# Experts' weights in 256 x 1024 tiles, split whole, with products and evictions over two PSUM banks

## Chip, cores and metric

One core of a Trainium2 chip runs one program of two transformer blocks. The metric is the device time of one execution in microseconds; less is better. Three runs of the kernel before are shown, and one execution was profiled.

## What is computed

512 tokens of width 1024, float32, go through two blocks. The first has a recurrence, an attention and a layer of 32 experts; each token goes to its four best ones. Of an expert, the part that matters here is this:

```python
def expert_block(args):
    tok, gate, e = args
    xb = xt[tok]
    hid = xb @ w1[e] + b1[e]
    glu = jnp.minimum(hid[:, :D_FF_EXPERT], SWIGLU_LIMIT)
    lin = jnp.clip(hid[:, D_FF_EXPERT:], -SWIGLU_LIMIT, SWIGLU_LIMIT)
    act = glu * jax.nn.sigmoid(SWIGLU_ALPHA * glu) * (lin + 1.0)
    return (act @ w2[e] + b2[e]) * gate[:, None]
```

`w1[e]` is 1024 x 2048: its first 1024 columns give the gated half, the others the linear half. `w2[e]` is 1024 x 1024. Results go back to their tokens, summed. The second block is a convolution, a sparse attention and a feed-forward layer; the change leaves its code alone.

## The kernel before, in words

**Precision.** A float32 product is made of three: weights and activations are split in a high part in a shorter format and a low part, the rest, and `mm3` (L99) multiplies high by high, high by low and low by high. For weights, `split` (L104, L105) is a cast on ACT into `wh` and a subtraction on DVE, or on POOL where it is told so, into `wl`.

**Experts' stage** (`phase_b`, L991). The 12 MiB of an expert come in 12 chunks of 1 MiB: eight of `w1` and four of `w2`. A chunk is 512 rows by 512 columns, held as a raw tile `wraw` of 128 partitions by 4 k by 512. `weights` (L953) lists all 384 chunks in the order of their products: an expert's first layer, then the second layer of the expert before. In the first layer it takes gated and linear columns in turn: 512 gated columns (two chunks), 512 linear ones, then the other 512 of each.

For chunk n the loop at the end of `phase_b` splits chunk n + 3 (`ahead`), issues the load of the chunk that takes its raw tile (8 of them), makes the twelve products of chunk n, and then runs the steps that were put behind n with `after`. PE, ACT, DVE and SP keep the order in which the program is written here. `wsplit` (L112) cuts a chunk in `self.parts` = PB = 2 pieces of 128 x 1024, and there are `nhl` = 8 half tiles `wh` and `wl` each. A chunk's twelve products go to one PSUM bank: `hid` has four banks, `y` two, `tr` two.

**Steps of an expert** (`plan`, L1077; b is its first chunk, y0 the first of its second layer). The gather of the next expert's rows (`xg`) goes out behind b, and eight transposes (`turn`) stand behind b+6 and their two parts `xt` (high on ACT, low on DVE) behind b+8 as two pieces of 128 x 384. `swiglu` stands behind b+4 and b+8: for 512 columns a clip of the gated part, its activation on ACT, a clip of the linear part and their product, all 96 x 512. The result `ln` is turned in two groups of four transposes behind b+11 and b+13, with parts `at` behind b+12 and b+14. `finish` (behind y0+4) weighs the result into `ys` in two pieces, and POOL scatters the rows into `acc`. Experts 30 and 31 have steps of their own (`L30`, `LS`).

**Before the stage** `phase_r` (L736) multiplies by `w_out`, normalises (`rst`, `rsy`, `h2r`), and routes the tokens with many small DVE operations (`oh`, `pos`, `rowi`). In the same time the first three chunks of experts' weights are cast on ACT and subtracted on POOL, so that they are ready when the stage begins.

**Block 2**, which the prediction uses for comparison, makes its products with the same `mm3`: those named `mm` and `mu` in runs of 24 into one bank, and those named `ro` (`rows_out`, L1694) token tile by token tile, two k and so six products into a tile's bank, then six into the next one's.

## Time and profile before

| | |
|---|---|
| runs of the kernel before | 2618.61, 2621.24 and 2624.76 us, median 2621.24 |
| span of the profiled execution | 2621.5 us; the profile gives no other time for it |
| PE busy | 2522.1 us, 96% |
| DVE busy | 1853.1 us, 71% |
| ACT busy | 1385.9 us, 53% |
| mean granted clock of PE | 0.965 |
| bytes of weights of the experts | 384 loads of 1024 KB |

The span reaches from the first instruction to the last of one execution. It is 0.3 us above the median of the runs, so terms that are worked out on it can be set against the median directly. Busy is time in which an engine runs an instruction other than one that moves registers, signals or starts transfers.

### The profile page before, as it was taken

The numbers are of one execution on the slowest core, as the hardware profiler recorded it, in microseconds if no ns is written. First come the engines' busy times: TensorE is split into PE (matmuls) and PEld (weight loads), VectorE is DVE, ScalarE is ACT, GpSimd is POOL, SyncE is SP. The second block draws the span as 40 slices with busy tenths as digits, with TensorE's granted clock in tenths as the row PEclk, the third lists the DMA queues.
The fourth block names the chain that finished last, engine by engine and source line by source line (L and its number), as shares of the span: only waits on it lengthen the run. The fifth ranks groups of instructions, "written<-read, shape, count | busy, mean of one in ns | idle before, by whom it ended". The sixth has DMA issues, their size and how long they took to land. (4 is left out here: it accounts for less than half of the span.)

```text
span 2621.5 us, 33210 instructions
## 1 busy us (share of the span) xinstructions
PE 2522.1 (96%) x12362; PEld 1774.2 (68%) x12362; DVE 1853.1 (71%) x2631; ACT 1385.9 (53%) x1952; POOL 336.2 (13%) x316
## 2 busy tenths in 40 slices
PE   6999998879999999999999999997999999899999
PEld 2567765656666666666666666666777678688887
DVE  3346556679999999999999999996666643555522
ACT  2333455347777777677767776764445532322221
POOL 2000222214211111111121111121100000000000
PEclk7899899889999999999999999998999999899999
DMA  8473000669999999999999999984421132333332
GB/s 275 122 223 79 17 1 0 235 235 326 345 369 349 356 348 355 351 353 355 350 354 351 354 351 355 348 268 109 105 57 49 33 89 73 105 97 97 93 95 70
DMA packets 371566, 556.75 MB, mean 212 GB/s; under 512 B 13138, under 2 KB 153501, under 8 KB 371401
## 3 DMA queue, kind: packets, MB, share of 16 engines
q1 hardware_dynamic: 359808, 518.81, 58.1%
q0 software_dynamic: 11120, 34.68, 6.2%
q8 instruction: 98, 1.61, 0.3%
q10 hardware_dynamic: 473, 1.11, 0.1%
q14 instruction: 67, 0.55, 0.1%
HBM read 534.06 MB, written 20.48 MB: 212 GB/s over the span
## 5 line engine op out<-in xcount | busy, mean ns | idle before, releaser
L105 DVE TENSOR_TENSOR wl<-wraw,wh 128x1024 fp32r<-128x1024 f32 (+2 forms) x974 | 1093.5, 1159 | 297.9 <-ACT wh L104 278.7
L104 ACT CAST wh<-wraw 128x1024 fp32r<-128x1024 f32 (+1 forms) x980 | 950.7, 997 | 637.4 <-PE mm L96 232.8
L96 PE MATMUL hid<-wh,xt 128*96 128x512 f32 x2048 | 676.5, 398 | 0.0
L96 PEld LDWEIGHTS hid<-wh,xt 128*96 128x96 f32 x2048 | 331.0, 162 | 151.7 <-issue 9.9
L96 PE MATMUL hid<-wl,xt 128*96 128x512 f32 x1024 | 404.6, 395 | 0.0
L96 PE MATMUL y<-wh,at 128*96 128x512 f32 x960 | 314.7, 398 | 0.0
L96 PE MATMUL mm<-hH,wh 128*128 128x512 f32 x624 | 255.0, 409 | 6.9 <-ACT wh L104 3.5
L96 PE MATMUL mm<-hL,wh 128*128 128x512 f32 x624 | 252.5, 405 | 0.0
L96 PE MATMUL mm<-hH,wl 128*128 128x512 f32 x624 | 251.0, 402 | 0.0
L1209 POOL DMA_INDIRECT acc<-ys,tli x30 | 154.3, 5145 | 517.7 <-DVE ys L1118 499.0
L96 PEld LDWEIGHTS y<-wh,at 128*96 128x96 f32 x960 | 154.9, 161 | 78.1 <-issue 14.4
L96 PEld LDWEIGHTS hid<-wl,xt 128*96 128x96 f32 x1024 | 165.6, 162 | 59.5
L96 PE MATMUL y<-wl,at 128*96 128x512 f32 x480 | 189.1, 394 | 0.0
L96 PEld LDWEIGHTS mm<-hH,wh 128*128 128x128 f32 x624 | 119.1, 191 | 43.4 <-issue 5.7
L96 PEld LDWEIGHTS mm<-hH,wl 128*128 128x128 f32 x624 | 119.0, 191 | 30.3 <-issue 2.6
L96 PEld LDWEIGHTS mm<-hL,wh 128*128 128x128 f32 x624 | 119.1, 191 | 29.2 <-issue 3.0
L74 ACT ACTIVATE gl<-gl 96x512 f32<-96x512 f32 x64 | 40.5, 632 | 131.3 <-DVE gl L1057 131.3
L96 PEld LDWEIGHTS y<-wl,at 128*96 128x96 f32 x480 | 77.5, 161 | 29.0
L1036 POOL DMA_INDIRECT xg<-h2d,tli x32 | 30.8, 963 | 432.4 <-PE tr L1044 427.3
L96 PE MATMUL mu<-hL,wh 128*128 128x512 f32 x176 | 70.2, 399 | 0.0
L96 PE MATMUL mu<-hH,wh 128*128 128x512 f32 x176 | 69.3, 394 | 0.0
L96 PE MATMUL mu<-hH,wl 128*128 128x512 f32 x176 | 69.0, 392 | 0.0
(554 smaller groups left out, 3384.9 us busy)
## 6 DMA issues: line engine op xcount, KB each, us to landing
wraw<-in_exp_w_dram SPq DMA_DIRECT2D x384, 1024.0 KB
wraw<-in_w_in_dram SPq DMA_DIRECT2D x62, 512.0 KB
wraw<-in_ada_w_dram SPq DMA_DIRECT2D x48, 512.0 KB
wraw<-in_w_ffn_in_dram SPq DMA_DIRECT2D x44, 512.0 KB
wraw<-in_w_ffn_out_dram SPq DMA_DIRECT2D x22, 512.0 KB
wraw<-in_w_out_dram SPq DMA_DIRECT2D x4, 1024.0 KB
wraw<-in_w_o_dram SPq DMA_DIRECT2D x8, 512.0 KB
acc<-zf SPq DMA_DIRECT2D x1, 2432.0 KB
```

The costliest lines, as they stand in the source:

```text
L74: ins = self.nc.scalar.activation(out, in_, func, **kw)
L96: self.nc.tensor.matmul(out, l, r, start=start, stop=stop, skip_group_check=True)
L104: self.nc.scalar.copy(h, src)
L105: (eng or self.nc.vector).tensor_sub(l, src, h.bitcast(F32))
L1036: self.gathered = nc.gpsimd.indirect_dma_start(out=xg, out_offset=None, in_=self.h2d, in_offset=bass.IndirectOffsetOnAxis(ap=self.tli[:, e ...
L1209: self.nc.gpsimd.indirect_dma_start(out=self.acc, out_offset=bass.IndirectOffsetOnAxis(ap=idx, axis=0), in_=ys, in_offset=None, compute_op ...
```

## The change

Loads: experts 0 to 29 (`OLD` = 30) take chunks of 256 rows by 1024 columns, a raw tile of 128 x 2 x 1024. First come the four chunks of the gated half, then the four of the linear half, then the four of the second layer of the expert before. Experts 30 and 31 keep the old form and order of chunks.

Splits: PB is 1, so a chunk is split whole, 128 x 2048 at a time, into four tiles of twice the size; `ahead` stays 3. This also holds for the first three chunks on POOL, for `w_out` in `phase_r`, and for experts 30 and 31.

Products: for each of two k, three products into one bank and three into the other, in PSUM tiles of two banks (pool `psp`: one `tr`, two `hid`, one `y`).

Evictions: one operation over both banks. The clip and activation of the gated half stand behind b+4, the linear half's clip and the product behind b+8, both 96 x 1024. `ln` is turned whole behind b+11, and its parts, 128 x 768, stand behind b+12. `xt`'s parts are 128 x 768 too, and `ys` is 96 x 1024 in one. Biases are split in three pieces instead of five (`BS`), and the rows of the gate go to one pair. The old pool `psb` is opened after the loop. The diff, without the lines that are only comments:

```diff
 GO = 0
+OLD = 30
...
-PB = 2
+PB = 1
...
-MB = dict(xg=1,xt=1,at=1,gl=2,ln=2,ys=1,raw=7,hl=4)
+MB = dict(xg=1,xt=1,at=1,gl=1,ln=1,ys=1)
...
-BS = [0,2,4,6,8,10]
+BS = [0,1,3,10]
...
-        L1 = lambda e: [(e, 1, hb, m, kh) for hb in range(2) for m in range(2) for kh in range(2)]
-        L2 = lambda e: [(e, 2, kh, cb, 0) for kh in range(2) for cb in range(2)]
+        L1 = lambda e: [(e, 1, i) for i in range(8)]
+        L2 = lambda e: [(e, 2, i) for i in range(4)]
         seq = self.seq = []
         for e in range(NE):
             seq += L1(e) + (L2(e - 1) if e else [])
...
     def load(self, n):
         if n < len(self.seq):
-            e, layer, u, v, kh = self.seq[n]
-            if layer == 1:
-                src = self.a["exp_w1"][0][e, 512 * kh:512 * kh + 512, 512 * u + D * v:512 * u + D * v + 512]
+            e, layer, i = self.seq[n]
+            w = self.a["exp_w1" if layer == 1 else "exp_w2"][0][e]
+            if e < OLD:
+                v, kq = divmod(i, 4)
+                src, shape = w[256 * kq:256 * kq + 256, D * v:D * v + D], [128, 2, D]
             else:
-                src = self.a["exp_w2"][0][e, 512 * u:512 * u + 512, 512 * v:512 * v + 512]
+                hb, m, kh = (i // 4, i // 2 % 2, i % 2) if layer == 1 else (i % 2, 0, i // 2)
+                c0 = 512 * hb + D * m
+                src, shape = w[512 * kh:512 * kh + 512, c0:c0 + 512], [128, 4, 512]
             two = n % RAW >= self.nraw
-            w = self.raw[n] = (self.wp2 if two else self.wp).tile([128, 4, 512], F32, name="wraw", tag="wraw",
+            w = self.raw[n] = (self.wp2 if two else self.wp).tile(shape, F32, name="wraw", tag="wraw",
                                                                   bufs=RAW - self.nraw if two else self.nraw)
             self.nc.sync.dma_start(w, src.rearrange("(k p) c -> p k c", p=128))
...
-        psum = self.pool(PS, "psb", space=PSUM)
-        P = lambda tag, bufs: psum.tile([128, 512], F32, name=tag, tag=tag, bufs=bufs)
-        T_ = lambda tag, n=512: bp.tile([C, n], F32, name=tag, tag=tag, bufs=MB[tag])
+        PP = ExitStack()
+        pairs = self.pool(PP, "psp", space=PSUM)
+        P2 = lambda tag: pairs.tile([128, 2, 512], F32, name=tag, tag=tag, bufs=2 if tag == "hid" else 1)
+        T_ = lambda tag: bp.tile([C, D], F32, name=tag, tag=tag, bufs=MB[tag])
...
-        def turn(src, b, c0):
-            p = P("tr", 2)
-            for k in range(4):
-                nc.tensor.transpose(p[:, k * C:(k + 1) * C], src[:, c0 + k * 128:c0 + (k + 1) * 128], self.ident[:C, :C])
-            return p[:, 0:4 * C].rearrange("p (k c) -> p k c", c=C), slice(4 * b, 4 * b + 4)
-        def parts(t, dst, scale=1.0):
-            pv, ks = t
-            self.act(dst[0][:, ks, :], pv, AF.Copy, scale=scale)
-            nc.vector.scalar_tensor_tensor(dst[1][:, ks, :], pv, scale, dst[0][:, ks, :].bitcast(F32), op0=OP.mult, op1=OP.subtract)
+        def turn(src, p, b0, nb):
+            for k in range(4 * b0, 4 * (b0 + nb)):
+                nc.tensor.transpose(p[:, k // 4, k % 4 * C:(k % 4 + 1) * C], src[:, k * 128:(k + 1) * 128], self.ident[:C, :C])
+            return p
+        def parts(p, dst, b0, nb, scale=1.0):
+            pv = p[:, b0:b0 + nb, 0:4 * C]
+            h, l = (t[:, 4 * b0:4 * (b0 + nb), :].rearrange("p (b k) c -> p b (k c)", b=nb) for t in dst)
+            self.act(h, pv, AF.Copy, scale=scale)
+            nc.vector.scalar_tensor_tensor(l, pv, scale, h.bitcast(F32), op0=OP.mult, op1=OP.subtract)
...
+        def glu(gl, pg):
+            nc.vector.tensor_scalar(gl, flat(pg), 7.0, None, op0=OP.min)
             self.act(gl, gl, AF.Silu, scale=1.702)
-            ln = T_("ln")
-            nc.vector.tensor_scalar(ln, pl[:C], 7.0, -7.0, op0=OP.min, op1=OP.max)
+        def lin(ln, pl, gl):
+            nc.vector.tensor_scalar(ln, flat(pl), 7.0, -7.0, op0=OP.min, op1=OP.max)
             self.last = nc.vector.scalar_tensor_tensor(ln, ln, 1.0, gl, op0=OP.add, op1=OP.mult)
-            return ln
+        def swiglu(e, u):
+            if not u:
+                X["gl"], X["ln"] = T_("gl"), T_("ln")
+            cs, p = slice(512 * u, 512 * u + 512), X["hid", e, u]
+            glu(X["gl"][:, cs], p[:, 0])
+            lin(X["ln"][:, cs], p[:, 1], X["gl"][:, cs])
...
-            b, y0 = at_[(e, 1, 0, 0, 0)], at_[(e, 2, 0, 0, 0)]
+            b, y0 = at_[(e, 1, 0)], at_[(e, 2, 0)]
             if e + 1 < NE:
                 after(b, keep(("xg", e + 1), lambda: gather(e + 1)))
                 n = b + XN if e == NE - 2 else b + 6
+                after(n, keep(("tx", e + 1), lambda: turn(X["xg", e + 1], P2("tr"), 0, 2)))
+                after(n + 1 if e == NE - 2 else max(min(at_[e + 1, 1, 0], b + 12) - ahead - 1, b + 7),
+                      lambda: (X.__setitem__(("xt", e + 1), pair("at" if e == NE - 2 else "xt")),
+                               parts(X["tx", e + 1], X["xt", e + 1], 0, 2)))
+            if e < OLD:
+                after(b + 4, lambda: (X.__setitem__("gl", T_("gl")), glu(X["gl"], X["hid", e, 0])))
+                after(b + 8, lambda: (X.__setitem__("ln", T_("ln")), lin(X["ln"], X["hid", e, 1], X["gl"])))
+                after(b + 11, keep("t", lambda: turn(X["ln"], P2("tr"), 0, 2)))
+                after(b + 12, lambda: (X.__setitem__(("at", e), pair("at")), parts(X["t"], X["at", e], 0, 2, 1 / 1.702)))
+            else:
+                steps = LS if e == NE - 1 else L30
+                after(b + 4, lambda: swiglu(e, 0))
+                after(b + steps[0], lambda: swiglu(e, 1))
                 for q in range(2):
-                    after(n, keep(("tx", e + 1, q), lambda q=q: turn(X["xg", e + 1], q, 512 * q)))
-                after(n + 1 if e == NE - 2 else max(min(at_[e + 1, 1, 0, 0, 0], b + 12) - ahead - 1, b + 7),
-                      lambda: (X.__setitem__(("xt", e + 1), pair("at" if e == NE - 2 else "xt")),
-                               [parts(X["tx", e + 1, q], X["xt", e + 1]) for q in range(2)]))
-            steps = LS if e == NE - 1 else L30 if e == NE - 2 else (8, 11, 12, 13, 14)
-            after(b + 4, keep(("ln", 0), lambda: swiglu(*X["hid", e, 0])))
-            after(b + steps[0], keep(("ln", 1), lambda: swiglu(*X["hid", e, 1])))
-            for q in range(2):
-                after(b + steps[1 + 2 * q], keep(("t", q), lambda q=q: turn(X["ln", q], q, 0)))
-                after(b + steps[2 + 2 * q], lambda q=q: (q or X.__setitem__(("at", e), pair("xt" if e >= NE - 2 else "at")),
-                                                         parts(X["t", q], X["at", e], 1 / 1.702)))
+                    after(b + steps[1 + 2 * q], keep("t", lambda q=q: turn(X["ln"], X["t"] if q else P2("tr"), q, 1)))
+                    after(b + steps[2 + 2 * q], lambda q=q: (q or X.__setitem__(("at", e), pair("xt")),
+                                                             parts(X["t"], X["at", e], q, 1, 1 / 1.702)))
...
-            ys = T_("xg" if e == NE - 2 else "ys", D)
-            for cb in range(2):
-                weigh(ys[:, 512 * cb:512 * cb + 512], e, cb)
+            ys = T_("xg" if e == NE - 2 else "ys")
+            weigh(ys, e, flat(X["y", e]))
...
-            e, layer, u, v, kh = seq[n]
+            e, layer, i = seq[n]
             if layer == 1:
-                if u == 0 and v == 0 and kh == 0:
+                if i == 0:
                     plan(e)
-                if v == 0 and kh == 0:
-                    X["hid", e, u] = [P("hid", 4), P("hid", 4)]
-                p, xt, bias = X["hid", e, u][v], X["xt", e], b1s[:, D * v + 512 * u:D * v + 512 * u + 512]
+                if i % 4 == 0:
+                    X["hid", e, i // 4] = P2("hid")
+                p, xt, b0 = X["hid", e, i // 4], X["xt", e], b1s
             else:
-                if u == 0 and v == 0:
-                    X["y", e] = [P("hid", 4) if e >= NE - YH else P("y", 2) for _ in range(2)]
-                p, xt, kh, bias = X["y", e][v], X["at", e], u, b2s[:, 512 * v:512 * v + 512]
+                if i == 0:
+                    X["y", e] = P2("hid" if e >= NE - YH else "y")
+                p, xt, b0 = X["y", e], X["at", e], b2s
             w = hl.pop(n)
-            for k in range(4):
-                kk = 4 * kh + k
-                self.mm3(p[:C], (xt[0][:, kk, :], xt[1][:, kk, :]), w[k], kk == 0, False)
-            if kh:
-                mm(p[:C], e2[:, e:e + 1].to_broadcast([64, C]), bias, False, True)
+            if e < OLD:
+                v, kq = divmod(i, 4)
+                todo_ = [(2 * kq + k, j, [t[:, 512 * j:512 * j + 512] for t in w[k]], D * v + 512 * j)
+                         for k in range(2) for j in range(2)]
+            else:
+                u, j, kh = (i // 4, i // 2 % 2, i % 2) if layer == 1 else (0, i % 2, i // 2)
+                todo_ = [(4 * kh + k, j, w[k], 512 * u + D * j if layer == 1 else 512 * j) for k in range(4)]
+            for kk, j, wk, c0 in todo_:
+                self.mm3(p[:C, j], (xt[0][:, kk, :], xt[1][:, kk, :]), wk, kk == 0, False)
+                if kk == KD - 1:
+                    mm(p[:C, j], e2[:, e:e + 1].to_broadcast([e2.shape[0], C]), b0[:, c0:c0 + 512], False, True)
```

Three places where instructions move.

POOL, where the first three chunks are split (`wl<-wraw,wh`; behind them the transfer of the normalised rows to `h2d` and the first gather `xg`). Before:

```order
L105 TENSOR_TENSOR wl<-wraw,wh 128x1024 x6
L882 DMA h2d<-h2r 128x1024 x2
L1036 DMA xg<-h2d,tli 96x1024
L1106 CAST tlc<-tli 96x1
L1036 DMA xg<-h2d,tli 96x1024 x3
```

Now:

```order
L106 TENSOR_TENSOR wl<-wraw,wh 128x2048 x3
L883 DMA h2d<-h2r 128x1024 x2
L1043 DMA xg<-h2d,tli 96x1024
L1126 CAST tlc<-tli 96x1
L1043 DMA xg<-h2d,tli 96x1024 x3
```

Six subtractions of 128 x 1024 have become three of 128 x 2048; what stands behind them is the same.

ACT in `phase_r`, second half of the routing (`h2r` sums of squares, `rsy` the root, `gt` the gates, `wh` the cast of the third chunk). Before:

```order
L888 COPY h2T<-tr 128x512
L74 ACTIVATE h2r,ss_4170<-x 128x512
L104 CAST wh<-wraw 128x1024
L74 ACTIVATE rsy<-rsv 128x1
L74 ACTIVATE rsy<-rsy 128x1
L104 CAST wh<-wraw 128x1024
L888 COPY h2T<-tr 128x512 x2
L74 ACTIVATE h2r,ss_4294<-x 128x512
```

Now:

```order
L889 COPY h2T<-tr 128x512
L75 ACTIVATE h2r,ss_4154<-x 128x512
L75 ACTIVATE rsy<-rsv 128x1
L75 ACTIVATE rsy<-rsy 128x1
L105 CAST wh<-wraw 128x2048
L889 COPY h2T<-tr 128x512 x2
L75 ACTIVATE h2r,ss_4270<-x 128x512
```

Half of the third chunk's cast stood ahead of the two `rsy`; now the whole cast stands behind them.

DVE, one expert in the middle of the stage (`ys` the weighing, `at` and `xt` the low parts, `gl` and `ln` the clips and the product). Before:

```order
L1118 SCALAR_TENSOR_TENSOR ys<-y,tlg,g2b 96x512 x2
L1050 SCALAR_TENSOR_TENSOR at_9326<-tr,at_9325 128x384
L105 TENSOR_TENSOR wl<-wraw,wh 128x1024 x4
L1050 SCALAR_TENSOR_TENSOR at_9326<-tr,at_9325 128x384
L105 TENSOR_TENSOR wl<-wraw,wh 128x1024 x4
L1057 TENSOR_SCALAR gl<-hid 96x512
L1060 TENSOR_SCALAR ln<-hid 96x512
L1061 SCALAR_TENSOR_TENSOR ln<-ln,gl 96x512
L105 TENSOR_TENSOR wl<-wraw,wh 128x1024 x8
L1050 SCALAR_TENSOR_TENSOR xt_9539<-tr,xt_9538 128x384 x2
L1057 TENSOR_SCALAR gl<-hid 96x512
L1060 TENSOR_SCALAR ln<-hid 96x512
```

Now:

```order
L1139 SCALAR_TENSOR_TENSOR ys<-y,tlg,g2b 96x1024
L1057 SCALAR_TENSOR_TENSOR at_10439<-tr,at_10438 128x768
L106 TENSOR_TENSOR wl<-wraw,wh 128x2048 x4
L1065 TENSOR_SCALAR gl<-hid 96x1024
L106 TENSOR_TENSOR wl<-wraw,wh 128x2048 x4
L1057 SCALAR_TENSOR_TENSOR xt_10607<-tr,xt_10606 128x768
L1069 TENSOR_SCALAR ln<-hid 96x1024
L1070 SCALAR_TENSOR_TENSOR ln<-ln,gl 96x1024
L106 TENSOR_TENSOR wl<-wraw,wh 128x2048 x4
```

A piece is twice as long and there are half as many; the clip of the gated half stands alone, four chunks ahead of the linear half's clip and the product, and the turned `at` comes in one piece behind `ys`.

## Rows read from the trace of the kernel before

**Rows 1.** The page, its head and the first row of its part 1: busy us and share.

```profile
span 2621.5 us, 33210 instructions
...
PE 2522.1 (96%) x12362; PEld 1774.2 (68%) x12362; DVE 1853.1 (71%) x2631; ACT 1385.9 (53%) x1952; POOL 336.2 (13%) x316
```

**Rows 2.** Table by windows, core 0: window, its us, busy us of each engine, clock, DMA.

```profile
700.00:800.00 100.00, 100.00 (x442) 65.69 (x440) 93.60 (x97) 71.28 (x80) 20.45 (x5) 1.00 1.05 367
```

**Rows 3.** List of waits, 700 to 1700 us: us in total, times, longest us.

```profile
ACT wh L104 <- PE hid L96: 140.3, 290, 1.0
ACT gl L74 <- DVE gl L1057: 102.4, 52, 2.1
```

**Rows 4.** Timeline of PE, two experts' turns: start us, us, operation.

```profile
1027.65 0.82 PE L1044 MATMUL tr<-ident,xg 96*128 96x96 f32 x8
1028.26 0.45 PE L96 MATMUL hid<-wh,xt 128*96 128x512 f32 x1
...
1065.71 0.82 PE L1044 MATMUL tr<-ident,xg 96*128 96x96 f32 x8
```

**Rows 5.** The chain that ended last, block 2: start us, us, what.

```profile
2273.10 5.60 PE mm L96 x24
...
2497.10 119.73 PE ro L96 x528
```

**Rows 6.** Groups by line and form, 700 to 1700 us: busy us, mean ns of one.

```profile
L105 DVE TENSOR_TENSOR wl<-wraw,wh 128x1024 fp32r<-128x1024 f32 x634 | 745.2, 1221 | 70.8 <-ACT wh L104 66.1
L104 ACT CAST wh<-wraw 128x1024 fp32r<-128x1024 f32 x633 | 643.0, 1048 | 187.6 <-PE hid L96 140.3 <-ACT wh L104 36.1 <-PE y L96 9.7
...
L1061 DVE SCALAR_TENSOR_TENSOR ln<-ln,gl 96x512 f32<-96x512 f32 x52 | 35.8, 688 | 5.4
...
L74 ACT ACTIVATE gl<-gl 96x512 f32<-96x512 f32 x52 | 32.9, 632 | 102.4 <-DVE gl L1057 102.4
...
L1050 DVE SCALAR_TENSOR_TENSOR at<-tr,at 128x384 fp32r<-128x384 f32 x54 | 29.3, 543 | 0.0
...
L74 ACT ACTIVATE at<-tr 128x384 fp32r<-128x384 f32 x54 | 26.0, 482 | 0.0
```

**Rows 7.** Timeline of POOL, 511 to 536 us.

```profile
512.48 10.29 POOL L105 TENSOR_TENSOR wl<-wraw,wh 128x1024 fp32r<-128x1024 f32 x4 [1.83 <-ACT wh L104]
527.73 4.82 POOL L105 TENSOR_TENSOR wl<-wraw,wh 128x1024 fp32r<-128x1024 f32 x2 [4.95 <-ACT wh L104]
```

**Rows 8.** Timeline of DVE, 511 to 537 us.

```profile
520.56 2.23 DVE L847 TENSOR_TENSOR pos<-tf,pos 128x4 f32<-128x4 f32 x1
...
527.48 0.16 DVE L847 TENSOR_TENSOR pos<-tf,pos 128x4 f32<-128x4 f32 x1
...
528.03 2.22 DVE L260 TENSOR_TENSOR rst<-rsy 128x1 f32<-128x1 f32 x1
530.28 2.29 DVE L261 TENSOR_TENSOR rst<-rst,rsv 128x1 f32<-128x1 f32 x1
...
534.31 1.23 DVE L881 TENSOR_TENSOR h2r<-h2r,s 128x1024 f32<-128x1024 f32 x1
```

**Rows 9.** Timeline of ACT, 511 to 537 us.

```profile
511.35 1.05 ACT L104 CAST wh<-wraw 128x1024 fp32r<-128x1024 f32 x1 [1.08 <-PE o L96]
```

**Rows 10.** Timeline of PE, the first products of the stage.

```profile
558.21 0.74 PE L96 MATMUL hid<-wh,xt 128*96 128x512 f32 x1
558.75 0.63 PE L96 MATMUL hid<-wl,xt 128*96 128x512 f32 x1
559.17 1.05 PE L96 MATMUL hid<-wh,xt 128*96 128x512 f32 x2
```

**Rows 11.** Timeline of PE, expert 2's turn.

```profile
609.47 0.55 PE L1044 MATMUL tr<-ident,xg 96*128 96x96 f32 x4 [1.17 <-DVE at L1050]
```

**Rows 12.** Timeline of all engines, end of the stage.

```profile
1769.93 0.55 DVE L1050 SCALAR_TENSOR_TENSOR xt<-tr,xt 128x384 fp32r<-128x384 f32 x1
...
1771.69 0.62 PE L96 MATMUL hid<-wh,xt 128*96 128x512 f32 x2
```

More of the change, by code (lines that the diff above doesn't have):

```diff
@@ L1005, in phase_b @@
         bp = self.pool(ES, "moe", side="right")
[L1006 to L1008 removed]
+        PP = ExitStack()
+        pairs = self.pool(PP, "psp", space=PSUM)
+        P2 = lambda tag: pairs.tile([128, 2, 512], F32, name=tag, tag=tag, bufs=2 if tag == "hid" else 1)
+        T_ = lambda tag: bp.tile([C, D], F32, name=tag, tag=tag, bufs=MB[tag])
         braw = {}
         def bias_load():
[L1013 to L1015 removed]
+            for n, (src, c0, tag) in enumerate((("exp_b1", 0, "gl"), ("exp_b1", D, "ln"), ("exp_b2", 0, "ys"))):
+                t = T_(tag)
                 for h in range(2):
[L1017 to L1018 removed]
+                    nc.sync.dma_start(t[32 * h:32 * h + 32], a[src][0, :, c0:c0 + D])
+                braw[n] = t, (b1s if n < 2 else b2s)[:, c0:c0 + D]
         def bias_split(n):
@@ L1025, in gate_rows @@
         def gate_rows():
+            p = P2("tr")
             for j in range(2):
-                p = P("tr", 2)
-                mm(p, self.ones[32 * j + 64:32 * j + 65, :], self.mod[2][32 * j + 64:32 * j + 65, :])
-                nc.scalar.copy(g2[:, 512 * j:512 * j + 512], p[:C])
+                mm(p[:, j], self.ones[32 * j + 64:32 * j + 65, :], self.mod[2][32 * j + 64:32 * j + 65, :])
+            nc.scalar.copy(g2, p[:C].rearrange("p j c -> p (j c)"))
         self.table("silu_and_others")
@@ L1102, in onehot @@
         def onehot():
-            io, t = T_("gl"), bp.tile([C, 1], F32, name="tlc")
+            io, t = T_("gl")[:, 0:T], bp.tile([C, 1], F32, name="tlc")
             nc.gpsimd.iota(io, pattern=[[1, T]], base=0, channel_multiplier=0, allow_small_or_imprecise_dtypes=True)
@@ L1112, in last @@
                 X["ys"] = self.wp.tile([C, 4, 512], F32R, name="ysp", tag="wraw", bufs=self.nraw)
-            ys = T_("ln")
-            weigh(ys, NE - 1, cb)
-            self.split(X["ys"][:, cb], X["ys"][:, 2 + cb], ys)
-        def weigh(ys, e, cb):
-            nc.vector.scalar_tensor_tensor(ys, X["y", e][cb][:C], self.tlg[:, e:e + 1], g2[:, 512 * cb:512 * cb + 512],
-                                           op0=OP.mult, op1=OP.mult)
+                X["yr"] = T_("ln")
+            cs = slice(512 * cb, 512 * cb + 512)
@@ L1121, in finish, with weigh @@
+            weigh(X["yr"][:, cs], NE - 1, X["y", NE - 1][:C, cb], cs)
+            self.split(X["ys"][:, cb], X["ys"][:, 2 + cb], X["yr"][:, cs])
+        def weigh(ys, e, p, cs=slice(0, D)):
+            nc.vector.scalar_tensor_tensor(ys, p, self.tlg[:, e:e + 1], g2[:, cs], op0=OP.mult, op1=OP.mult)
         def finish(e):
-            ys = T_("xg" if e == NE - 2 else "ys", D)
-            for cb in range(2):
-                weigh(ys[:, 512 * cb:512 * cb + 512], e, cb)
+            ys = T_("xg" if e == NE - 2 else "ys")
+            weigh(ys, e, flat(X["y", e]))
@@ L1150, in phase_b @@
             bias_load()
-            for n in range(5):
+            for n in range(3):
                 after(BS[n], lambda n=n: bias_split(n))
-            after(BS[5], gate_rows)
+            after(BS[3], gate_rows)
             X["xg", 0], X["xt", 0] = gather(0), pair("xt")
@@ L1156, in phase_b @@
                 split(n, nc.gpsimd)
-            for q in range(2):
-                parts(turn(X["xg", 0], q, 512 * q), X["xt", 0])
+            parts(turn(X["xg", 0], P2("tr"), 0, 2), X["xt", 0], 0, 2)
             for n in range(len(seq)):
@@ L1174, in phase_b @@
         ES.close()
+        PP.close()
+        psum = self.pool(PS, "psb", space=PSUM)
+        P = lambda tag, bufs: psum.tile([128, 512], F32, name=tag, tag=tag, bufs=bufs)
         self.overflow(P)
```

12 lines of the change are left out of this document (2 added, 10 removed).

## The prediction

> **What bounds the kernel now.** I read the page first: PE is busy for 2522.1 of 2621.5 us, 96%; no other engine comes near [rows 1]. A share over the whole program says nothing of one stage, so the next view is the table by windows. The change lives in the experts' stage, which runs from about 558 to 1780 us, and there a window of 100 us has 100.00 us of PE at a granted clock of 1.00 (the 2.4 GHz level), with DVE at 94 and the DMA engines at 1.03 of their time [rows 2]. Three resources look full. The list of waits tells which of them is waited for. Between 700 and 1700 us it has no wait of PE for data and no wait for a transfer. ACT waits 290 times for PE to give back a split tile [rows 3]: the engines that prepare weights run ahead until the tiles are full, and then wait for PE. A full DMA share is a queue that is always fed, not a bound. So this stage costs what PE's instructions cost, and the questions are whether PE's list gets shorter, whether a product gets quicker or slower, and whether DVE or ACT, now with other piece sizes, ever comes late.
>
> PE's list of one expert is 144 products, six bias products and sixteen transposes. The transposes of two neighbouring experts start at 1027.65 and 1065.71 us, so an expert lasts 38.06 us and a chunk of twelve products 3.17 us on average [rows 4].
>
> **The change, part by part. Products over two banks.** Number and size of PE's instructions stay; what is new is that the bank changes after every three products instead of after twelve (or more). The rows that are nearest are in the chain of block 2: 528 products of `ro` in 119.73 us are 226.8 ns each, and in that loop the bank changes after every six; 24 products of `mm`, which stay much longer in one, are 5.60 us, 233 ns each [rows 5]. The engine pays nothing visible for a change of bank; I take 0. The ends: if all of the 6.5 ns between the two were due to banks, and the same fell to each of the 4320 products of experts 0 to 29, it would be -28 us; 5 ns lost at each of 1440 changes would be +7. That the two loops differ in much else (weights' width, other engines' load) is why neither end is my value.
>
> **Transposes in eights, biases one product earlier.** The same instructions stand grouped otherwise; the work of PE is equal, 0, between -0.3 and +0.3 us an expert by the 0.61 us from the eight transposes' start to the next product's [rows 4], which would be 9 us either way over 30 experts. I keep 0, since eight in one place already cost as much as two groups of four.
>
> **Splits in whole tiles.** DVE's time for one piece: 512 elements cost 688 ns and 1024 cost 1221 [rows 6], that is 1.04 ns an element, so 2048 are 1221 + 1024 x 1.04 = 2.29 us (ends: 2.24, and 2.44, twice a half). ACT: 632 ns for 512 and 1048 for 1024 give 0.81 ns an element, 1.88 us for 2048 (at most 2.10). The evictions over two banks are 96x1024: 688 + 533 = 1.22 us for each of the two clips, the product with the gate and `ys`; the turned parts, 128x768, 543 + 400 = 0.94 us on DVE and 0.80 on ACT. DVE per expert: 12 x 2.29 + 4 x 1.22 + 2 x 0.94 = 34.2 us of 38.06. DVE stays below PE, and its 94% falls to 90.
>
> What matters more is when a piece is ready. There are four whole tiles, as much memory as eight halves, so the cast for the chunk three ahead begins when PE leaves a tile, 3 x 3.17 = 9.5 us before that chunk's products. With nothing in the way the low part is ready after 1.88 + 2.29 = 4.2 us: 5.3 us to spare. Two places of an expert are tighter. After b+4, ACT's order puts the activation of the gated half behind DVE's clip, and the clip stands behind a whole subtraction: cast to 1.9, subtraction to 4.2, clip to 5.4, activation (about 1.05) to 6.4, next cast to 8.3, its subtraction to 10.6, needed at 12.7: 2.1 us to spare. After b+8, DVE does the turned `xt`, the clip and the product with the gate (0.94 + 1.22 + 1.22) between two subtractions: ready at 9.9, needed at 12.7, 2.8 to spare. Nothing reaches PE, so this term is 0; what covers it is those 2 us. The 102.4 us that ACT now waits for DVE's `gl` [rows 3] grow per wait and halve in number. Of the larger loads nothing is waited for today, and the bytes are the same.
>
> **The start.** Before the stage the first three chunks are cut with POOL doing the subtraction, beside DVE's routing work. The rows show a collision: POOL is at it for 10.29 and 4.82 us [rows 7], and inside these stretches DVE's operations with two inputs in SBUF stretch: `pos`, 0.16 us at 527.48, took 2.23 at 520.56, and two `rst` took 2.22 and 2.29 [rows 8], each about one POOL piece. With whole pieces POOL's are 4.8 us. The Trainium skill's page "SBUF — State Buffer" (section "SBUF: two separate sides") says that such a DVE operation and a GpSimd one that reads SBUF take a port pair as an exclusive lock for the whole instruction; the rows above agree with it, and by it a whole piece holds DVE off for up to twice as long at once, while sharing by bandwidth would leave this term near 0.
>
> First stretch: the first cast now needs a whole tile and starts about 1.4 us later than 511.35 [rows 9], ends 0.8 us later still, and POOL's two pieces end about 2.2 us after the old 522.77; DVE leaves the stretch that much later. Second stretch: ACT's order now has both `rsy` activations ahead of the whole cast, where one half stood before them. So the two `rst`, which lose 2.22 + 2.29 - 2 x 0.16 = 4.2 us today, run ahead of POOL. But POOL then starts about when `h2r` times `s` (1.23 us, at 534.31) is due, and may hold it for its 4.8 us. Held: +2.2 + 0.4 = +2.6; not held: +2.2 - 4.2 = -2.0. The two come within 0.1 us of a tie, and I think held is somewhat likelier, since POOL gets in between two DVE operations in the rows too (POOL's second piece starts between the two `rst`). I take +2.0, ends -2.0 and +2.6.
>
> **The first products** (558.21) come behind one ACT part of 0.80 us over all eight transposes instead of one of 0.48 over four: +0.5 us (0.3 to 1.1) [rows 10]. **A stall that goes:** at 609.47 PE waited for a `tr` bank [rows 11], where expert 2's transposes needed one that the turned `ln` still held. The turn is now whole after b+11, and its bank is read before the gather's turn is due: -1.4 us with the transposes' own slip. Late next would be the splits, and they have their 2 us. **The tail:** with experts 30 and 31 whole splits stand ahead of the small steps; the last low part was there at 1770.48 and products that use it begin some 1.4 us later [rows 12]; a half more ahead of it costs 0 to 1.5, I take +0.8.
>
> **Sum:** 0 + 0 + 0 + 2.0 + 0.5 - 1.4 + 0.8 = +1.9 us. The profiled execution spans 2621.5 us, 0.3 above the median of 2621.24, so the forecast is **2623 us**; the term is under 0.1% of the time. A measurement of this kernel can tell about 0.2%, 5.2 us, from no change.
>
> **Rivals.**
> - *Late splits (slower).* One mechanism: the chain clip, activation, cast, subtraction after b+4, which has 2.1 us to spare. For it: DVE would have two idle stretches less to catch up in, and the activation waits behind a piece of twice the length. Against it: waits of ACT for PE show that today's reserve is not used up. It decides once the chain takes 2.1 us more than worked out, for instance with pieces at 2.44 and 2.10 us (2 x 0.15 + 2 x 0.22 = 0.7 us) and 1.4 us of semaphores. Each 0.1 us beyond that costs 30 x 0.1 = 3 us; a lateness of 0.2 to 1 us gives 2629 to 2653. Chance 0.17.
> - *Quicker products (faster).* If the change of bank is what makes `ro` 226.8 ns, products fall from 233 towards that: -28 us, 2595; a third of it 2613. Against it: two loops are compared that differ in more. Chance 0.08.
> - *The start falls well (faster).* Not held, and first products on time: -2.0 + 0.3 - 1.4 + 0 = -3.1, 2618; it is inside the 0.2%. Part of the forecast's chance, 0.17 of it.
> - *The clock falls.* At the first products the clock was low: they start 0.54 and 0.42 us apart, against 0.23 later [rows 10]. If changing banks broke PE's run so that ten products of each expert went at that pace, 30 x 10 x 0.2 = 60 us, 2683. The windows say 1.00 throughout, and `ro` changes banks at full pace. Chance 0.03. The Trainium skill's page "TensorE: Matmul & The Clock Gate" (section "A second HAM failure mode: psum-queue depth-cycling") describes a kernel whose clock swung because PE idled a little between groups of products as it went round the banks; no run here shows that.
> - *It does nothing:* all terms 0, 2621.5; not to be told apart from the forecast, and counted with it.
>
> **How the numbers follow.** The forecast with its near cases (nothing, a start that falls well) has 0.69, late splits 0.17, quicker products 0.08, the clock 0.03, and bank changes that cost 5 ns each (+7 us) 0.03. Of the 0.69, 0.05 is for small gains that sum to over 5.2 us and 0.02 for small losses that do; of the late splits 0.03 is for a lateness so small that it lands inside. Faster: 0.08 + 0.05 = 0.13. Slower: 0.17 - 0.03 + 0.03 + 0.03 + 0.02 = 0.22. The same: 0.65. The range of 8 in 10 takes the forecast's ends (the start's -2.0 to +2.6, the tail, the first products: 2617 to 2626) and reaches to a third of the product gain below and to a lateness of about 0.4 us an expert above: 2613 to 2635.
>
> **What would show it.** Right: windows of 100 us between 700 and 1700 still with 100.00 of PE and transposes 38.0 us apart; `wl` 128x2048 near 2.29 us, `wh` near 1.88; no `tr` wait near 608; POOL's three pieces near 4.8 us with DVE operations of up to 4.8 us beside them; the first product within 3 us of 558.7. Wrong: PE waiting for `wl` or `wh` in the list of waits (late splits), an expert of 37.3 us or less (quicker products), or a granted clock below 1.00 after 600 us.

## The result, and the profile after

The changed kernel takes 2643.11 us (median of 4 runs, 2640.06 to 2646.94) against 2623.0 us before on the same chip (4 runs, 2618.61 to 2628.09): a ratio of 1.0079, 95% interval 1.0058 to 1.0100. It is slower by 15 to 26 us. The prediction was 2623, 2613 to 2635, "the same" at 0.65; it is wrong.

The page after, its head and the first row of part 1, against [rows 1]; then the table by windows, one row of the steady stage, against [rows 2]; then groups by line and form between 700 and 1700 us, against [rows 6]:

```profile
span 2638.1 us, 31763 instructions
...
PE 2526.6 (96%) x12362; PEld 1775.1 (67%) x12362; DVE 1795.2 (68%) x2061; ACT 1325.8 (50%) x1469; POOL 264.4 (10%) x313
```

```profile
700.00:800.00 100.00, 100.00 (x436) 65.48 (x435) 90.21 (x50) 64.95 (x39) 14.51 (x5) 1.00 1.00 369
```

```profile
L106 DVE TENSOR_TENSOR wl<-wraw,wh 128x2048 fp32r<-128x2048 f32 x316 | 712.3, 2286 | 122.0 <-ACT wh L105 120.3
L105 ACT CAST wh<-wraw 128x2048 fp32r<-128x2048 f32 x316 | 598.0, 1908 | 250.8 <-PE hid L97 118.2 <-PE y L97 103.6 <-issue 29.0
...
L75 ACT ACTIVATE gl<-gl 96x1024 f32<-96x1024 f32 x26 | 27.6, 1061 | 90.7 <-DVE gl L1065 90.7
```

The steady stage is as forecast: PE 100.00 of 100 us at a granted clock of 1.00, a whole subtraction 2286 ns (2.29 was worked out), a cast 1908 ns (1.88), an activation over two banks 1061, and DVE busy for 90 us of the window instead of 94. Yet the span is 16.6 us longer than the 2621.5 of before. So the loss is not in the steady part, and the next step is to cut the stage in pieces at marks that both programs have: the first of the eight transposes of an expert's gathered rows, and the first product behind the stage (`ysp`). PE's timeline before:

```profile
580.64 0.83 PE L1044 MATMUL tr<-ident,xg 96*128 96x96 f32 x8
...
607.80 0.49 PE L1044 MATMUL tr<-ident,xg 96*128 96x96 f32 x4
...
647.20 0.82 PE L1044 MATMUL tr<-ident,xg 96*128 96x96 f32 x8
...
1673.98 0.82 PE L1044 MATMUL tr<-ident,xg 96*128 96x96 f32 x8
...
1731.09 0.82 PE L1044 MATMUL tr<-ident,xg 96*128 96x96 f32 x8
...
1780.97 2.27 PE L96 MATMUL hid<-ysp,one 96*128 96x512 f32 x8 [2.39 <-issue]
```

and after:

```profile
583.66 0.82 PE L1050 MATMUL tr<-ident,xg 96*128 96x96 f32 x8
...
615.02 0.83 PE L1050 MATMUL tr<-ident,xg 96*128 96x96 f32 x8
...
653.12 0.82 PE L1050 MATMUL tr<-ident,xg 96*128 96x96 f32 x8
...
1681.78 0.82 PE L1050 MATMUL tr<-ident,xg 96*128 96x96 f32 x8
...
1745.96 0.82 PE L1050 MATMUL tr<-ident,xg 96*128 96x96 f32 x8
...
1798.07 2.12 PE L97 MATMUL hid<-ysp,one 96*128 96x512 f32 x8 [2.31 <-POOL cz L1518]
```

(At 607.80 only the first four of expert 2's transposes stand together, before the stall of [rows 11].) The differences of these starts, and three ways ahead of them, read from the same timelines:

| way | before | after | change |
|---|---|---|---|
| `w_out`'s first product (473.37; 474.66) to the last `tl` (550.41; 551.90) | 77.04 | 77.24 | +0.20 |
| last `tl` to the first turn (556.73; 558.88) | 6.32 | 6.98 | +0.66 |
| first turn to the first product (558.21; 561.32) | 1.48 | 2.44 | +0.96 |
| expert 1's turn to expert 2's | 27.16 | 31.36 | +4.20 |
| expert 2's to expert 3's | 39.40 | 38.10 | -1.30 |
| expert 3's to expert 30's, 27 experts | 1026.78 | 1028.66 | +1.88 |
| expert 30's to expert 31's | 57.11 | 64.18 | +7.07 |
| expert 31's to the first product behind the stage | 49.88 | 52.11 | +2.23 |

With -0.1 from the first product to expert 1's turn and -0.5 behind the stage these are +15.3 us; the other 1.3 us of the 16.6 fall ahead of `w_out`, in code that is the same. Two ways hold most of it.

**Expert 1.** PE's timeline after, around its first products:

```profile
588.52 0.47 PE L97 MATMUL hid<-wh,xt 128*96 128x512 f32 x1 [0.27 <-ACT xt L75]
588.83 0.40 PE L97 MATMUL hid<-wl,xt 128*96 128x512 f32 x1
591.37 0.71 PE L97 MATMUL hid<-wh,xt 128*96 128x512 f32 x2 [2.15 <-DVE xt L1057]
...
592.15 1.04 PE L97 MATMUL hid<-wh,xt 128*96 128x512 f32 x2
```

DVE's and then ACT's timeline there:

```profile
577.36 2.29 DVE L106 TENSOR_TENSOR wl<-wraw,wh 128x2048 fp32r<-128x2048 f32 x1
579.57 1.22 DVE L1065 TENSOR_SCALAR gl<-hid 96x1024 f32<-96x1024 f32 x1
583.76 6.69 DVE L106 TENSOR_TENSOR wl<-wraw,wh 128x2048 fp32r<-128x2048 f32 x3 [2.97 <-ACT wh L105]
590.37 0.95 DVE L1057 SCALAR_TENSOR_TENSOR xt<-tr,xt 128x768 fp32r<-128x768 f32 x1
```

```profile
580.87 1.06 ACT L75 ACTIVATE gl<-gl 96x1024 f32<-96x1024 f32 x1 [4.01 <-DVE gl L1065]
581.83 5.50 ACT L105 CAST wh<-wraw 128x2048 fp32r<-128x2048 f32 x3
587.65 0.81 ACT L75 ACTIVATE xt<-tr 128x768 fp32r<-128x768 f32 x1 [0.32 <-PE hid L97]
```

PE waits 2.15 us for the low part of `xt`, which DVE begins at 590.37, behind three whole subtractions (6.69 us). These were late because DVE had no cast to work on from 580.8 to 583.76: ACT stood 4.01 us waiting for the clip of the gated half, 579.57, itself behind a whole subtraction. That is the chain of the rival on late splits, but what it made late is the low part of `xt`, not a piece of weights. In the steady stage the pieces of weights have room: from 700 to 1660 us every whole subtraction ends at least 1.84 us before the first product that reads it starts, against the 2.1 worked out. The least of the whole stage is 0.78 us (a subtraction that ends at 675.63, its product at 676.41). Expert 0 has no second layer of an expert before it, so expert 1's `xt` is needed at chunk 8, not at chunk 12, right when the last product that uses the old `xt` is done; its parts stand behind chunk 7, and not behind b+8 as for the others. Behind the wait the products run at half pace: the pair at 592.15 takes 1.04 us where a pair at full clock takes 0.62 [rows 12]. Eight products start 0.43 us apart instead of 0.23, and the table by windows gives a granted clock of 0.50, the 1.2 GHz level:

```profile
593.00:594.00 1.00, 1.00 (x4) 0.70 (x3) 1.00 (x2) 0.00 (x0) 0.00 (x0) 0.50 0.99 397
```

Two waits of 0.27 and 2.15 us and eight products that cost 0.2 us more each are 4.0 of the 4.20 us.

**Expert 30.** PE's timeline, then DVE's:

```profile
1733.62 0.90 PE L1050 MATMUL tr<-ident,ln 96*128 96x96 f32 x4 [3.77 <-DVE xt L1057]
...
1735.18 1.05 PE L97 MATMUL y<-wh,at 128*96 128x512 f32 x2
```

```profile
1730.81 2.29 DVE L106 TENSOR_TENSOR wl<-wraw,wh 128x2048 fp32r<-128x2048 f32 x1 [1.10 <-ACT wh L105]
1733.02 0.55 DVE L1057 SCALAR_TENSOR_TENSOR xt<-tr,xt 128x384 fp32r<-128x384 f32 x1
```

The second four transposes of expert 30's `ln` wait 3.77 us for the low part made of the first four. In the kernel before the two groups lay in two `tr` banks with no tie between them. Now both lie in one tile of two banks, and PE waits until DVE has read the first half, although the second half goes to the other bank. That the program as built ties a tile as a whole is a reading of this wait; e1 tests it. The part stands behind a whole subtraction. The products behind it run at half pace again (two in 1.05 us; 11 of them, table by windows):

```profile
1735.00:1736.00 1.00, 1.00 (x3) 0.58 (x3) 1.00 (x2) 0.05 (x1) 0.00 (x0) 0.50 0.98 371
```

### The profile page after: what moved, and what is told of

It is laid out like the page before. It is cut to its first block, busy times and chain, and to the rows that moved or that the text cites. A ratio compares the mean times of both kernels' runs of the same rounds, so it can differ in the third digit from the quotient of the medians.

```text
span 2638.1 us, 31763 instructions
## 1 busy us (share of the span) xinstructions
PE 2526.6 (96%) x12362; PEld 1775.1 (67%) x12362; DVE 1795.2 (68%) x2061; ACT 1325.8 (50%) x1469; POOL 264.4 (10%) x313
## 5 line engine op out<-in xcount | busy, mean ns | idle before, releaser
L106 DVE TENSOR_TENSOR wl<-wraw,wh 128x2048 fp32r<-128x2048 f32 (+3 forms) x589 | 1056.2, 1815 | 376.5 <-ACT wh L105 360.0
L105 ACT CAST wh<-wraw 128x2048 fp32r<-128x2048 f32 (+3 forms) x592 | 897.3, 1528 | 722.1 <-PE mm L97 241.4
L1237 POOL DMA_INDIRECT acc<-ys,tli x30 | 59.9, 1996 | 573.3 <-DVE ys L1139 572.7
L1043 POOL DMA_INDIRECT xg<-h2d,tli x32 | 48.7, 1523 | 462.7 <-PE tr L1050 457.3
L75 ACT ACTIVATE gl<-gl 96x1024 f32<-96x1024 f32 (+1 forms) x34 | 34.4, 1010 | 119.5 <-DVE gl L1065 119.5
```

The lines of the kernel that those rows point to most:

```text
L75: ins = self.nc.scalar.activation(out, in_, func, **kw)
L105: self.nc.scalar.copy(h, src)
L106: (eng or self.nc.vector).tensor_sub(l, src, h.bitcast(F32))
L1043: self.gathered = nc.gpsimd.indirect_dma_start(out=xg, out_offset=None, in_=self.h2d, in_offset=bass.IndirectOffsetOnAxis(ap=self.tli[:, e ...
L1237: self.nc.gpsimd.indirect_dma_start(out=self.acc, out_offset=bass.IndirectOffsetOnAxis(ap=idx, axis=0), in_=ys, in_offset=None, compute_op ...
```

## The experiments

All are judged by the same marks; a whole program's time scatters by more than most of these effects (below). The ways in us, from expert 1's turn on:

| kernel | 1 to 2 | 2 to 3 | 3 to 30 | 30 to 31 | 31 to end | sum | ratio to before, 95% |
|---|---|---|---|---|---|---|---|
| before | 27.16 | 39.40 | 1026.78 | 57.11 | 49.88 | 1200.3 | |
| changed | 31.36 | 38.10 | 1028.66 | 64.18 | 52.11 | 1214.4 | 1.0079 (1.0058 to 1.0100) |
| e5, changed again | 31.35 | 38.11 | 1028.66 | 64.22 | 52.10 | 1214.4 | 1.0069 (1.0045 to 1.0093) |
| e1, own pair | 32.23 | 38.10 | 1028.66 | 57.85 | 52.16 | 1209.0 | 1.0025 (1.0007 to 1.0042) |
| e2, halves | 27.91 | 38.10 | 1028.66 | 59.03 | 50.76 | 1204.5 | 1.0016 (0.9993 to 1.0039) |
| e3, parts first | 27.88 | 38.11 | 1028.66 | 64.24 | 52.05 | 1210.9 | 1.0047 (1.0026 to 1.0068) |
| e4, before aligned | 27.19 | 39.47 | 1028.40 | 57.17 | 49.93 | 1202.2 | 1.0015 (1.0003 to 1.0027) |
| e6, two mended | 27.90 | 38.10 | 1028.66 | 57.87 | 52.14 | 1204.7 | 1.0021 (1.0002 to 1.0040) |
| e7, mended, halves | 27.90 | 38.10 | 1028.66 | 57.72 | 50.76 | 1203.1 | 1.0032 (1.0007 to 1.0057) |
| e8, before, whole | 31.19 | 42.48 | 1026.72 | 57.21 | 51.06 | 1208.7 | 1.0033 (1.0012 to 1.0054) |
| e9, all mended | 27.19 | 38.10 | 1028.66 | 57.72 | 49.83 | 1201.5 | 1.0010 (0.9990 to 1.0030) |
| e10, six a bank | 27.18 | 38.02 | 1027.67 | 57.73 | 49.81 | 1200.4 | one run, 2631.96 us |

**e1: a pair of its own for expert 30's second turn.**

```diff
-turn(X["ln"], X["t"] if q else P2("tr"), q, 1)
+turn(X["ln"], P2("hid" if q and e == NE - 2 else "tr"), q, 1)
```

> The changed kernel with one edit: the second half of expert 30's turned product goes to a free PSUM pair of `hid` instead of the second bank of the `tr` pair that holds the first half. Theory A (three local waits: the start, expert 1's `xt`, expert 30's turn, and the steady stage innocent): PE's wait of 3.8 us before the second four transposes at about 1733 goes, with the products at half clock that follow it, so that the way from expert 30's gather turn to expert 31's is about 58 us instead of 64.2, and the program is 6 us shorter than the changed one (about 1.0055 of before instead of 1.0079). Theory B (whole splits are late at each of these places, whatever the bank): the transposes then wait for something else, and that way stays within 2 us of 64.2.

PE's timeline of e1:

```profile
1735.56 0.49 PE L1050 MATMUL tr<-ident,ln 96*128 96x96 f32 x4
...
1738.72 0.55 PE L1050 MATMUL hid<-ident,ln 96*128 96x96 f32 x4
...
1748.58 0.82 PE L1050 MATMUL tr<-ident,xg 96*128 96x96 f32 x8
```

The second group starts at 1738.72 with nothing waited for, and the way to expert 31 is 57.85 us, 6.3 shorter. The tie between the two halves of the pair was the loss: A holds for this place and B falls. Whole splits, still there, don't make PE wait at that place by themselves.

**e2: splits in halves.** The edit is `PB = 2`.

> The changed kernel with PB = 2: every split in two halves again, eight half tiles, all else as changed (chunks of 256 x 1024, alternating banks, evictions over two banks, pairs). Theory A: the start goes back by about 1.5 us (POOL's pieces begin when a half tile is free), expert 1's `xt` comes earlier because the chain of cast, subtraction, clip, activation moves in pieces of half the length (of the 4.2 us lost between the turns of experts 1 and 2 at least 2 come back), and expert 30's turn still waits, 2 to 4 us, since the pair and the order stay. Sum: 4 to 7 us shorter than the changed kernel. Theory B (whole splits are the cause of everything): all of it comes back, at most 3 us more than before. Theory C (products and evictions over two banks are the cause): nothing comes back, within 2 us of the changed kernel.

PE's timeline of e2, the second turn of expert 30 and expert 31's turn:

```profile
1732.00 0.55 PE L1050 MATMUL tr<-ident,ln 96*128 96x96 f32 x4 [1.07 <-DVE xt L1057]
...
1741.88 0.82 PE L1050 MATMUL tr<-ident,xg 96*128 96x96 f32 x8
```

Expert 1 gets 3.45 us back, the tail 1.35, and the wait at expert 30 shrinks to 1.07 us where 2 to 4 were expected: with halves a tile is free earlier, so the cast and the subtraction ahead of the part are earlier too. DVE's subtraction ahead of the part waits 0.25 us for its cast, where it waits 1.10 in the changed kernel. 9.9 us of the 14.1 in these ways come back: more than A's sum, less than B's all, and C falls. The 1.5 us that A expected at the start don't come: from `w_out`'s first product to the last `tl` it is 77.09 us, 0.2 less than changed.

**e3: expert 1's parts ahead of chunk 10's split.**

```diff
 for n in range(len(seq)):
+    if n == 7:
+        products(n)
+        for f in todo.pop(n):
+            f()
     split(n + ahead)
-    products(n)
+    if n != 7:
+        products(n)
```

> The changed kernel with one edit in the order: behind chunk 7 the parts of expert 1's `xt` stand ahead of the split of chunk 10 on ACT and DVE, not behind it. Theory A: PE's wait of 2.5 us at 588.8 shrinks to about 1 us (the high part's 0.8 us on ACT and the low part's 0.95 on DVE remain, as xt has one buffer), fewer products at half clock follow, and the way between the turns of experts 1 and 2 falls from 31.4 us to 28 to 29. Theory B': the subtraction of the chunk, not the low part, is what PE really lacks there, and the wait stays at 2 us or more, then named for `wl`.

PE's timeline of e3:

```profile
591.94 0.71 PE L97 MATMUL hid<-wh,xt 128*96 128x512 f32 x2 [0.28 <-DVE xt L1057]
...
614.00 0.83 PE L1050 MATMUL tr<-ident,xg 96*128 96x96 f32 x8
```

The wait for the low part is 0.28 us instead of 2.15, and the way to expert 2 is 27.88 us, less than even expected, because no stretch at half pace follows this wait. So the order on DVE was the loss, not the subtraction that PE would need next. (On ACT the order changes too, but in both traces ACT's high part starts when PE releases the old `xt`.)

**e4: does the place of the stationary tiles set the pace?** On the kernel before: `bb.tile([128, 16], F32, name="pad")` ahead of the experts' pool.

> The kernel before with one edit: an unused tile of 64 bytes a partition ahead of the experts' pool, so that the stationary tiles `xt` and `at` begin at a multiple of 128 bytes instead of 64 bytes behind one. This asks what sets a product's pace. Theory D (the 231 ns of the experts' products against the 226.8 of `ro` come from where the stationary tile lies): an expert lasts about 37.4 us instead of 38.06 and the program is 15 to 22 us shorter. Theory E (the pace has another cause, banks or load of other engines): within 2 us of before.

Experts did not get quicker: 1028.40 us for 27 of them, 38.09 each, 0.06 more than before. D falls, if the tile moved the others as meant: no trace shows addresses. The program's ratio is 1.0015, and the ways are 1.9 us longer in all, so nothing here speaks against E. The gap between 231 and 226.8 ns stays open.

**e5** is the changed kernel once more.

> The changed kernel once more, unedited, so that it stands on the same chip beside the mended ones. Every theory: between 1.005 and 1.010 of before; in the trace the way between the turns of experts 1 and 2 is 31.4 us, from expert 30's turn to expert 31's 64.2 us, the rest of the stage as in the first trace within 0.3 us.

Its ways agree with the first trace within 0.04 us, so the marks can mostly be trusted to a tenth. The one exception is e1's way from 1 to 2, 0.87 us longer with nothing edited there. PE's wait for the low part is even shorter there, 1.93 us, but 13 products follow it at half pace instead of 8. The wait ends at 599.24, and e1's table by windows still has a granted clock of 0.50 at 604 us:

```profile
604.00:605.00 1.00, 1.00 (x4) 0.65 (x3) 0.00 (x0) 1.00 (x1) 0.00 (x0) 0.50 1.04 414
```

So the price of a wait at this place is good to about 1 us, not to a tenth.

**e6** has the edits of e1 and e3 together.

> The changed kernel with both edits that helped: expert 30's second turn in a pair of its own, and expert 1's parts ahead of the split of chunk 10. Theory A (separate local waits): the gains add, 6.3 + 3.5 = 9.8 us less than the changed kernel, with whole splits kept: ratio to before 1.001 to 1.004. Theory B (one lateness of whole splits that only shows at one place or another): the second mend gives less than half of its own gain, and new waits of PE of over 1 us turn up elsewhere in the stage.

The ways sum to 1204.7, 9.7 us below the changed kernel: the two gains add, and no other wait of PE in the stage grows by more than 0.2 us. A holds, B falls.

**e7** is e6 with `PB = 2`.

> As the one before, and PB = 2 on top, so that only the chunks' form, the alternating banks and the evictions over two banks are left of the change. Theory A: the tail gives back another 1 to 2 us and expert 1's wait a few tenths; what stays against before is 0.6 us at the gather, 0.9 at the first products, up to 2 us in the steady stage, less the 1.3 us of the stall at 608: within 3 us of before (0.999 to 1.0015). Theory C (banks and wide evictions cost something themselves): at least 6 us slower than before.

The tail gave back 1.4, expert 1's wait nothing (27.90 us in both). The ways are 2.8 us over before, and with 0.96 at the first product and 0.4 at the gather that is 4.2 us, more than the 3 expected; the measured ratio lies above the forecast too, with 1.0015 inside its interval. By the marks C's 6 us are not there. The ratio's interval, 1.8 to 15 us, can't exclude them.

**e8: whole splits alone.** The kernel before with `PB = 1`.

> The kernel before with PB = 1 alone: splits whole, all else old (two `tr` banks, evictions of 512, chunks of 512 x 512). Theory A: no pair couples the two turns of expert 30, so the way from expert 30's turn to expert 31's grows by at most 2 us (57.1 before, 64.2 changed); between the turns of experts 1 and 2 some 1 to 4 us are lost, since the parts stand behind three whole subtractions; the tail loses 1 to 2; 3 to 7 us slower than before in all. Theory B (whole splits are all of it): 12 to 18 us slower, with 64 us at expert 30.

PE's timeline of e8, the waits at experts 1 and 2:

```profile
585.23 0.93 PE L96 MATMUL hid<-wh,xt 128*96 128x512 f32 x2 [1.69 <-DVE xt L1050]
...
612.56 0.68 PE L1044 MATMUL tr<-ident,xg 96*128 96x96 f32 x4 [2.63 <-DVE at L1050]
```

Whole splits alone cost 4.0 us at expert 1 and 1.2 in the tail, as A has it, and nothing at expert 30, where two `tr` banks are free of each other. What neither theory had: the old stall of [rows 11] grows from 1.17 to 2.63 us, since the part it waits for now stands behind whole subtractions. With products at a granted clock of 0.50 behind it (614 to 616 us) the way from expert 2 to 3 is 3.1 us longer. Hence 8.3 us instead of 3 to 7. The changed kernel, whose turn is whole, has no such stall.

**e9: all mended.** On e7: the last expert's result in two pairs, and the parts of the first two `xt` in halves.

```diff
-X["y", e] = P2("hid" if e >= NE - YH else "y")
+X["y", e] = Two(P2("hid"), P2("hid")) if e == NE - 1 else P2("hid" if e >= NE - YH else "y")
...
-parts(turn(X["xg", 0], P2("tr"), 0, 2), X["xt", 0], 0, 2)
+halves(turn(X["xg", 0], P2("tr"), 0, 2), X["xt", 0])
```

> The two mends and PB = 2, and on top: the last expert's result in two pairs instead of the two banks of one, and the parts of the first two experts' `xt` in two halves of 384 columns as before. Theory A (each loss has a place of its own, and PSUM pairs that two engines take turns on are two of these places): from the stage's first turn to the first product 1.5 us again (2.4 in the changed kernel), between the turns of experts 1 and 2 27.2 us (27.9 without halves), from expert 31's turn to the products behind the stage 49.9 us (50.8 without the second pair). From expert 1's turn to that point then 1201.5 to 1202.5 us, against 1200.3 before and 1214.4 changed, and the whole program within 3 us of before. Theory B (other places turn late when these are mended): that sum stays over 1203.

The sum is 1201.5, the tail 49.83 and experts 1 to 2 27.19, as A has it. The tail's last part was a second tie in a pair. In PE's timeline of the changed kernel the turn at 1784.49 waits 0.64 us, a low part 0.25, and at 1792.34 the second half of the last result waits for the weighing of the first. The first two are gone with halves in e7; the third, 0.84 us, is the tie: it is in e7 still, and gone in e9.

```profile
1784.49 0.55 PE L1050 MATMUL tr<-ident,ln 96*128 96x96 f32 x4 [0.64 <-DVE ovr L1246]
...
1792.34 0.48 PE L97 MATMUL hid<-wh,xt 128*96 128x512 f32 x1 [0.84 <-DVE ln L1139]
```

Only the first product is a miss: 2.12 us behind the turn, not 1.5. The whole turn of eight stands in one pair, and the first part waits for all of it.

**e10: six products a bank, then six in the other.**

```diff
-for k in range(2) for j in range(2)]
+for j in range(2) for k in range(2)]
```

> As e9_all_mended, and of the two banks one gets six products in a row and then the other, instead of three and three. It asks what makes an expert of the changed kernel 38.10 us where it was 38.03. Theory F (changes of bank): 24 instead of 48 changes an expert, and the way from expert 3's turn to expert 30's falls from 1028.7 by about 0.9 us. Theory G (something else, the same in both): it stays within 0.2 us.

The way over 27 experts falls by 0.99 us, as F has it. It is one run, but this way was 1028.66 us in all eight traces with three and three. With 24 changes of bank fewer an expert, 648 in all, one costs 1.5 ns, if the changes are what costs: the order of the k changes with them, and the two weren't parted. The mended kernel's ways are then those of before, 1200.4 against 1200.3 us; no version here beats before.

## Why the prediction was wrong

- *What bounds the stage*: right. PE is full, windows and pace are unchanged, and the lighter DVE and ACT buy nothing.
- *Splits in whole tiles, "nothing reaches PE, so this term is 0"*: **the step that failed.** The sizes were right within 30 ns. The reserve of 2.1 us was worked out for pieces of weights, for an expert in the middle, and taken for all. There it held, with 1.84 us measured from 700 us on. That `xt`'s own low part could come late was not asked. For expert 1 it is due four chunks earlier, and DVE made it behind three whole subtractions: +4.2 us. e3 shows that the order there is the cause, e8 that whole splits do it alone.
- *The tail, "0 to 1.5"*: **failed**, +9.3 us. The term counted only a half piece more ahead of a part, and looked at expert 31's part [rows 12], where 2.2 us were lost, not at expert 30's turn, where 7.1 were. What was missed is that two banks became one tile: PE's write to one half waits for a reader of the other. e1 gives 6.3 us back and e9's second pair 0.9; the whole pieces are 1.2 to 1.4. Some 0.6 to 0.8 us from expert 30 to 31 stay in every mended kernel, with no cause known.
- *The start, +2.0*: measured +0.20. POOL's timeline after, and DVE's beside it:

```profile
515.72 9.57 POOL L106 TENSOR_TENSOR wl<-wraw,wh 128x2048 fp32r<-128x2048 f32 x2 [4.11 <-ACT wh L105]
534.40 4.54 POOL L106 TENSOR_TENSOR wl<-wraw,wh 128x2048 fp32r<-128x2048 f32 x1 [9.11 <-issue]
```

```profile
517.26 3.59 DVE L863 TENSOR_TENSOR x<-x,xt 128x512 f32<-128x512 f32 x1
...
521.41 3.91 DVE L842 SCALAR_TENSOR_TENSOR rowi<-pos,ef 128x4 int32<-128x4 f32 x1
...
531.19 0.16 DVE L261 TENSOR_TENSOR rst<-rsy 128x1 f32<-128x1 f32 x1
...
533.28 1.22 DVE L882 TENSOR_TENSOR h2r<-h2r,s 128x1024 f32<-128x1024 f32 x1
537.22 0.69 DVE L862 TENSOR_TENSOR xt<-o,g 128x512 f32<-128x512 f32 x1 [2.71 <-PE o L97]
```

  The first stretch came about as worked out: DVE is held for longer at once (3.59 and 3.91 us), `rowi` ends with the second piece, and DVE leaves the stretch 1.9 us later than before (2.2 forecast), both times counted from `w_out`'s first product. But the second stretch fell to the not-held side: `rst` is 0.16 us, and `h2r` times `s` at 533.28 runs before POOL begins at 534.40. By what the Trainium skill's page "SBUF — State Buffer" says (section "SBUF: two separate sides"), the one that starts first has the ports. The rows agree: `h2r` times `s` takes 1.22 us, as it does when POOL is at rest. The tie I saw went the other way. Yet the -2.0 of that side didn't come either, and this the prediction had wrong: it took DVE alone for the path. DVE is 2.3 us ahead of before at 533.28, and then waits 2.71 us for PE's `o`. PE had waited 2.03 us for DVE's `B` at the end of the first stretch, and its first products of `o` behind that wait start 0.43 us apart, at a granted clock of 0.50 from 528 to 530 us. So what DVE gained is lost on PE. PE's timeline after:

```profile
526.39 0.89 PE L97 MATMUL tl<-B,A 128*96 128x64 f32 x8 [2.03 <-DVE B L849]
```

- *The first products, +0.5*: measured +0.96, inside its ends, as PE's timeline after shows (0.90 us of it a wait for ACT's whole part):

```profile
558.88 1.54 PE L1050 MATMUL tr<-ident,xg 96*128 96x96 f32 x8 [6.60 <-DMA xg<-h2d,tli]
561.32 0.74 PE L97 MATMUL hid<-wh,xt 128*96 128x512 f32 x1 [0.90 <-ACT xt L75]
```

  Ahead of it the gather lands 0.66 us later, which no term had. All traces with chunks of 256 x 1024 show it (6.8 to 7.3 us from the last `tl`, against 6.2 to 6.4 with the old chunks), so it goes with the loads' form or with something else that these kernels share; neither was tried alone.
- *The stall that goes, -1.4*: measured -1.30; right.
- *Products over two banks, 0*: at most 1.5 ns a change (e10), about 1.7 of the +1.88 us if old chunks have some 8 changes an expert. Inside its bounds.
- *Rival "late splits"*: its band of 2629 to 2653 holds the result, but that is luck: as a lateness of every expert it didn't happen. It came at the edges, once, and by the tie of banks. The rivals of quicker products and of the clock in the steady stage are out (1.00 throughout); the half clock behind each long wait, a cost that I had only as a rival, made a wait of 3.77 us cost 6.3. A small misreading changes nothing: the row of [rows 2] gives the DMA engines 1.05 of their time, not 1.03.

The medians differ by 20.1 us, the two profiled executions by 16.6; the rest isn't attributed, and the last section says why it can't be from single profiles.

## What to carry to other kernels

A reserve that is worked out for the middle of a loop says nothing of its first and last rounds: walk the order there by itself, chunk by chunk. Joining two PSUM banks in one tile halves the number of evictions but ties the halves together, as this program is built, so that whoever writes one waits for whoever reads the other; keep separate tiles where two engines take turns (e1: 64.2 us fall to 57.9). And a stage that is full of one engine gains nothing when the others get lighter.
